# Hybrid pooling and RG-LRU block with a mixture of experts: the last two experts added by slots on chip, the other rows read back and stored under them

## The chip, the cores and the metric

The kernel runs on one core of a Trainium2 chip. The metric is the device time in microseconds (us) of one execution; the median of three runs of the kernel before is 685.51 us (685.21 to 685.75).

## The reference

One decoder block on 512 tokens of 1024 channels, all in float32. The first part (norm, input projection, pooling mixer, recurrence, gates, output projection) gives `x`; the change does not touch it. What it touches is the mixture of experts and the last norm. Of 4 groups of 4 experts each token gets the best group and in it the best 2 experts, with the weights `comb` (512 by 16); an expert goes from 1024 channels to 512 and back. `rms_norm` is x times rsqrt(mean(x*x) + 1e-6) times the factors.

```python
def hier_moe(h, rg_w, rg_b, re_w, re_b, e_gate, e_up, e_down):
    ...
    comb = jnp.einsum('tk,tke->te', w2, jax.nn.one_hot(ids, N_EXP, dtype=jnp.float32)).astype(h.dtype)
    y = jnp.zeros_like(xt)
    for e in range(N_EXP):
        he = jax.nn.silu(xt @ e_gate[e]) * (xt @ e_up[e])
        y = y + comb[:, e:e + 1] * (he @ e_down[e])
    return y.reshape(b_, s_, d_)

def reference(...):
    ...
        x = x + (g_a * y_a + g_b * y_b) @ w_out[l]
        h2 = rms_norm(x, norm2_g[l])
        x = x + hier_moe(h2, ...)
    return rms_norm(x, norm_f_g)
```

## The kernel before, in words

**Slots.** Each expert has 128 slots, one per partition. `rows[:, e]` holds the token of each slot (a number from 512 up for an empty one, which every indirect transfer with its bounds check leaves out), `wslot[:, e]` its weight. With 512 tokens, 2 experts each and 16 experts, a slot list holds 64 tokens on average. `h2d` in HBM holds the normed rows, `xd` in HBM is the accumulator that the block's `x` is written to and every expert's result is added to.

**An expert.** GpSimd gathers the expert's rows of `h2d` into `xg` (`gather`, L507). TensorE transposes them (`x_parts`, L776); a float32 is carried as a high and a low part (`evac4`, L502: ACT copies the high part, DVE subtracts for the low), and each product is three matmuls (`tok_mm`, L784). `gate_half` and `up` (L840, L823) make 128x512 results, `hidden` (L793) the silu product, `h_parts` (L799) its transposed parts `ht`, `down` (L831) the 128x1024 result, which ACT scales into `yt`. `scatter_add` (L805) adds `yt` into `xd` by an indirect DMA of GpSimd. The loop at L849 interleaves: expert `e`'s gate halves stand around expert `e-1`'s `h_parts`, then `down(e-1)`, then `up(e)`.

**Weights.** They come in chunks of 1 MB in the order of the list `chunks` (L122 to L131) over SyncE's queue, three in flight (`load_raw`, L138). A chunk is split in two halves into high and low parts (`split`, L150: ACT copies, DVE subtracts), always three halves ahead of their use (`weights`, L159). Raw chunks and split halves share the 20 buffers of the tag `b8`; one half is one buffer, and one raw chunk too.

**Order.** The framework places instructions on each engine by a list: first what stands first in the program, as soon as its plan says it is ready. On an engine the order is then fixed, and each instruction waits in place for its semaphores. An `If` block is one unit in that list. Its body here (L881 to L934) works off experts with more than 128 tokens and is skipped with these inputs; every engine loads the count `nmi`, branches, and puts the semaphores of the skipped body right.

**The last two experts and the end.** Expert 14's second `down` half stands behind expert 15's `up` (L858 to L875), expert 14's scatter behind it. Then the overflow test (L880), then the read-back of all of `xd` into `xb` (L937 to L939), the load of the last norm's factors `gfb`, expert 15's `h_parts` and products (L944 to L951). Expert 15's result does not go through `xd`: a 0/1 matrix `back` (slots by tokens, L866 to L873) spreads it over the 512 rows by 16 matmuls, DVE adds them to `xb`, ACT makes sums of squares, GpSimd the power -0.5, and DVE (ACT and GpSimd for two parts) scales and hands each half row block to a store (L957 to L980).

Of the kernel before, what the change touches and what calls it, by code (L numbers as in the profile page):

```python
# [8 lines left out]
F32 = mybir.dt.float32  # L9
F32R = mybir.dt.float32r  # L10
# [7 lines left out]
P = 128  # L18
# [18 lines left out]
def tile_hybrid_block(  # L37
# [469 lines left out]
    def gather(idx, dst, n=S):  # L507
        return POOL.indirect_dma_start(  # L508
            out=dst, out_offset=None, in_=h2d[:n, :],
            in_offset=bass.IndirectOffsetOnAxis(ap=idx, axis=0),  # L510
            bounds_check=n - 1, oob_is_err=False).ins
# [335 lines left out]
    L = NE - 1  # L847
    hh = None
    for e in range(NE):  # L849
# [16 lines left out]
    toki = s2([P, S], I32, "toki")  # L866
    POOL.iota(toki, pattern=[[1, S]], base=0, channel_multiplier=0)
    tokf = s2([P, S], F32, "tokf")
    DVE.tensor_copy(tokf, toki)
    slf = tiny([P, 1], F32, "slf", 1)  # L870
    DVE.tensor_copy(slf, rows[:, L:L + 1])
    back = s2([P, S], F32R, "back")
    DVE.tensor_scalar(back, tokf, slf, None, op0=ALU.is_equal)  # L873
    for _ in part:
        pass  # L875
    for i in range(2):
        weights(c_d[L][i], 0, 0)


    n_max = nc.values_load(nmi[0:1, 0:1], min_val=0, max_val=S)  # L880
    with tc.If(n_max > P):  # L881
        emp = s2([P, S * NE // P], I32, "emp")
        POOL.iota(emp, pattern=[[1, S * NE // P // NE], [0, NE]], base=0, channel_multiplier=S // P)
        DVE.tensor_scalar(emp, emp, P - 1, None, op0=ALU.bitwise_and)
        DVE.tensor_scalar(emp, emp, S, None, op0=ALU.add)
        POOL.dma_start(tbl.rearrange("(p n) o -> p (n o)", p=P), emp)
        emw = s2([P, S * NE // P], F32, "emw")
        POOL.memset(emw, 0.0)
        POOL.dma_start(tblw.rearrange("(p n) o -> p (n o)", p=P), emw)
        ids = tiny([P, NT], I32, "ids", 1)  # L890
        POOL.iota(ids, pattern=[[P, NT]], base=0, channel_multiplier=1)
        adi = tiny([P, NT, 2], I32, "adi", 1)
        DVE.tensor_copy(adi, addr)
        for t in range(NT):
            for k in range(2):
                off = bass.IndirectOffsetOnAxis(ap=adi[:, t, k:k + 1], axis=0)
                POOL.indirect_dma_start(out=tbl, out_offset=off, in_=ids[:, t:t + 1], in_offset=None)
                POOL.indirect_dma_start(out=tblw, out_offset=off, in_=wtok[:, t, k:k + 1], in_offset=None)
        with tc.For_i(0, NE, 1) as ie:
            with tc.For_i(P, S, P) as iq:  # L900
                sl = const.tile([P, 1], I32, name="osl")
                SP.dma_start(sl, tbl.rearrange("(s n) o -> s (n o)", n=NE)[bass.ds(iq, P), bass.ds(ie, 1)])
                wsl = const.tile([P, 1], F32, name="owsl")
                SP.dma_start(wsl, tblw.rearrange("(s n) o -> s (n o)", n=NE)[bass.ds(iq, P), bass.ds(ie, 1)])
                og = s4([P, D], F32, "og")
                POOL.memset(og, 0.0)
                gather(sl, og)
                xt = b8([P, 2, KD, P], F32R, "xt_o")
                tb1 = bank("o_t")
                x_parts(og, xt, "o", tb1)  # L910
                r = b8([P, 4, 512], F32, "oraw")
                ow = [b8([P, 2, 2, 512], F32R, f"ow{i}") for i in range(2)]
                ht = s4([P, 2, 4, P], F32R, "ht_o")
                opg, opu = bank("opg"), bank("opu")

                def part(w, r0, c0):
                    src = w[bass.ds(ie, 1), r0:r0 + 512, c0:c0 + 512]
                    SP.dma_start(r, src.rearrange("o (k p) n -> p (o k) n", p=P))
                    for h in range(2):
                        split(r[:, 2 * h:2 * h + 2], ow[h][:, 0], ow[h][:, 1])  # L920
                    return lambda h: ow[h]

                for w, ps in ((e_gate, opg), (e_up, opu)):
                    for i in range(2):
                        tok_mm(ps, xt, 4 * i, part(w, 512 * i, 0), i == 0, i == 1)
                oh_ = hidden(opg, opu, "o")
                for q in range(4):
# [83 lines left out]
```

## Time and profile before

| | |
|---|---|
| median of three runs | 685.51 us (685.21 to 685.75) |
| the profiled execution's own time | 686.77 us |
| its span, first to last instruction | 684.9 us |
| TensorE (PE), busy share of the span | 95% |
| DVE | 73% |
| ACT | 63% |
| GpSimd (POOL) | 11% |
| mean granted TensorE clock | 0.978 |
| HBM read, written | 146.67 MB, 14.16 MB |

PE is TensorE's matmul, PEld its weight load, SP SyncE; a q behind an engine's name is its sequencer. A matmul's end is modelled, so a busy TensorE is read by the distance between starts, and by the shares of stretches rather than of the span. Rows of the chain give start, duration and what held the chain; rows of a line give duration (least/median/most, ns) and the first and last start; "idle before" names what the engine waited for.

### The profile page before, as it was taken

Reading aid. Unit: us, or ns where it says so; the run is one execution under the profiler, and the core shown is the slowest. Engines: PE = TensorE matmul, PEld = TensorE weight load, DVE = VectorE, ACT = ScalarE, POOL = GpSimd, SP = SyncE. Lnnn points to the kernel's source line nnn. Section 1 sums busy time; section 2 is a strip of 40 time slices with the busy share of each in tenths; the row PEclk is TensorE's granted clock in tenths of the full one; section 3 lists DMA queues with packets and bytes.
Section 4 is the critical chain, followed back from the end, with each engine's and each line's share of the span. In section 5 each row is a group of like instructions: output and inputs, shape, how many; then the busy total and the mean of one; then the engine's idle time right before and its main releaser. Section 6 shows DMA issues by size and latency. Waiting matters only on the chain. (4 is left out here: it accounts for less than half of the span.)

```text
span 684.9 us, 8419 instructions
## 1 busy us (share of the span) xinstructions
PE 650.5 (95%) x3044; PEld 528.2 (77%) x3044; DVE 501.8 (73%) x795; ACT 430.9 (63%) x581; POOL 76.5 (11%) x100
## 2 busy tenths in 40 slices
PE   4999999999999999999999999999999999999960
PEld 3788788888888888887777888777777778788850
DVE  5895689972233117657678999898888888889946
ACT  5689958661223224332135888888888888888913
POOL 3000000000100000001120112222222222211013
PEclk9999999999999999999987999999999999999995
DMA  6930321512307131697595899999999999999534
GB/s 202 331 115 1 128 72 35 211 63 76 114 2 250 57 122 68 242 345 263 175 359 185 283 351 350 354 337 339 332 345 346 341 337 340 335 331 344 206 102 162
DMA packets 88052, 153.23 MB, mean 224 GB/s; under 512 B 7249, under 2 KB 29893, under 8 KB 88008
## 3 DMA queue, kind: packets, MB, share of 16 engines
q1 hardware_dynamic: 81736, 138.98, 58.7%
q0 software_dynamic: 5824, 12.64, 6.7%
q10 hardware_dynamic: 448, 1.05, 0.4%
q8 instruction: 24, 0.39, 0.2%
q14 instruction: 20, 0.16, 0.1%
HBM read 146.67 MB, written 14.16 MB: 235 GB/s over the span
## 5 line engine op out<-in xcount | busy, mean ns | idle before, releaser
L152 DVE TENSOR_TENSOR w<-raw,w 128x1024 fp32r<-128x1024 f32 x248 | 293.4, 1220 | 67.4 <-ACT w L151 64.9
L151 ACT CAST w<-raw 128x1024 fp32r<-128x1024 f32 x248 | 249.1, 1051 | 57.3 <-DVE w L152 13.9
L789 PE MATMUL pg<-w,xt 128*128 128x512 f32 x128 | 53.2, 415 | 1.3
L789 PE MATMUL pu<-w,xt 128*128 128x512 f32 x128 | 51.3, 401 | 0.0
L790 PE MATMUL pu<-w,xt 128*128 128x512 f32 x128 | 50.9, 398 | 0.0
L790 PE MATMUL py<-w,ht 128*128 128x512 f32 x128 | 50.8, 397 | 0.0
L790 PE MATMUL pg<-w,xt 128*128 128x512 f32 x128 | 50.5, 394 | 0.0
L791 PE MATMUL pg<-w,xt 128*128 128x512 f32 x128 | 50.5, 394 | 0.0
L791 PE MATMUL pu<-w,xt 128*128 128x512 f32 x128 | 50.1, 392 | 0.0
L791 PE MATMUL py<-w,ht 128*128 128x512 f32 x128 | 49.9, 390 | 0.0
L508 POOL DMA_INDIRECT xg<-h_rows,rows x16 | 27.1, 1694 | 201.3 <-PE xtp L781 173.8
L789 PE MATMUL py<-w,ht 128*128 128x512 f32 x128 | 48.2, 391 | 1.0 <-ACT ht L504 1.0
L789 PEld LDWEIGHTS pg<-w,xt 128*128 128x128 f32 x128 | 24.3, 190 | 10.1 <-ACT w L151 5.9
L806 POOL DMA_INDIRECT x_acc<-y,rows x15 | 24.5, 1633 | 55.3 <-ACT y L836 51.6
L790 PEld LDWEIGHTS pg<-w,xt 128*128 128x128 f32 x128 | 24.4, 190 | 6.6 <-DVE w L152 0.7
L789 PEld LDWEIGHTS py<-w,ht 128*128 128x128 f32 x128 | 24.0, 188 | 6.2 <-ACT ht L504 1.3
L790 PEld LDWEIGHTS pu<-w,xt 128*128 128x128 f32 x128 | 24.1, 188 | 5.7 <-DVE w L152 0.2
L791 PEld LDWEIGHTS pg<-w,xt 128*128 128x128 f32 x128 | 24.3, 189 | 5.0
L791 PEld LDWEIGHTS py<-w,ht 128*128 128x128 f32 x128 | 24.1, 188 | 5.0 <-DVE ht L505 0.4
L791 PEld LDWEIGHTS pu<-w,xt 128*128 128x128 f32 x128 | 24.0, 188 | 4.7
L789 PEld LDWEIGHTS pu<-w,xt 128*128 128x128 f32 x128 | 24.0, 188 | 4.6
L790 PEld LDWEIGHTS py<-w,ht 128*128 128x128 f32 x128 | 24.1, 188 | 4.5
(303 smaller groups left out, 1408.9 us busy)
## 6 DMA issues: line engine op xcount, KB each, us to landing
raw<-in_exp_w_gate_dram SPq DMA_DIRECT2D x32, 1024.0 KB
raw<-in_exp_w_up_dram SPq DMA_DIRECT2D x32, 1024.0 KB
raw<-in_exp_w_down_dram SPq DMA_DIRECT2D x32, 1024.0 KB
raw<-in_w_in_dram SPq DMA_DIRECT2D x17, 1024.0 KB
raw<-in_proj_b_dram SPq DMA_DIRECT2D x4, 1024.0 KB
raw<-in_w_out_dram SPq DMA_DIRECT2D x4, 1024.0 KB
x_rows<-in_x_dram SPq DMA_DIRECT2D x4, 512.0 KB
xrow<-in_x_dram SPq DMA_DIRECT2D x4, 512.0 KB
```

Source lines behind the costliest of these rows:

```text
L151: ACT.copy(hi, r)
L152: DVE.tensor_tensor(lo, r, hi.bitcast(F32), op=ALU.subtract)
L508: return POOL.indirect_dma_start(out=dst, out_offset=None, in_=h2d[:n, :], in_offset=bass.IndirectOffsetOnAxis(ap=idx, axis=0), bounds_che ...
L789: PE.matmul(ps, hi, w[:, 0, k % 2, :], start=first and k == 0, stop=False)
L790: PE.matmul(ps, hi, w[:, 1, k % 2, :], start=False, stop=False)
L791: PE.matmul(ps, lo, w[:, 0, k % 2, :], start=False, stop=last and k == 3)
L806: POOL.indirect_dma_start(out=xd, out_offset=bass.IndirectOffsetOnAxis(ap=idx, axis=0), in_=src, in_offset=None, bounds_check=S - 1, oob_i ...
```

## The change

The weights of expert 14's second `down` half go back to their regular place. The overflow block moves, unchanged, into a function that is called in the loop at expert 14, behind `down(13)` and `next_x(15)` and ahead of `up(14)`. Behind it `read_back` loads the 512 rows of `xd` (experts 0 to 13 added) into `xb`, and gathers expert 14's and expert 15's rows of `xd` by their slots into `xz`. `rows_in_both` makes a 0/1 matrix `same` (slots of 14 by slots of 15 that hold one token) and `rows_m`, which is `rows` of expert 14 with the tokens that are in both lists moved out of bounds. Expert 14's result is kept on chip: added to its `xz` by GpSimd, and through four matmuls with `same` to expert 15's `xz`. Expert 15's up product goes in two column halves, its down product in two row halves between them. The 512 rows are normed and stored, behind the last split on ACT and DVE; then both `xz` are normed and stored over them by two indirect DMAs of GpSimd, which wait for the four row stores.

```diff
@@ chunks
-        if e == NE - 1:
-            late = chunks.pop()
         add_exp(c_u, e_up, e, False)
-    c_d[NE - 2][1] = len(chunks)
-    chunks.append(late)
     add_exp(c_d, e_down, NE - 1, True)
@@ split
+    latest = [None, None]
     def split(r, hi, lo):
-        ACT.copy(hi, r)
-        DVE.tensor_tensor(lo, r, hi.bitcast(F32), op=ALU.subtract)
+        latest[0] = ACT.copy(hi, r).ins
+        latest[1] = DVE.tensor_tensor(lo, r, hi.bitcast(F32), op=ALU.subtract).ins
@@ gather takes its source as src=h2d
@@ before the loop over the experts
+    def overflow():
+        n_max = nc.values_load(nmi[0:1, 0:1], min_val=0, max_val=S)
+        with tc.If(n_max > P):
...
+    def read_back():
+        xzt = b8([P, 2, D], F32, "xz")
+        POOL.memset(xzt, 0.0)
+        for i in range(2):
+            xb[i] = b8([P, 2, D], F32, f"xb{i}")
+        for t in range(NT):
+            SP.dma_start(xb[t // 2][:, t % 2, :], xd[t * P:(t + 1) * P, :])
+        for i in range(2):
+            xz[L - 1 + i] = xzt[:, i, :]
+            gather(rows[:, L - 1 + i:L + i], xz[L - 1 + i], src=xd)
+        gfb = const.tile([P, D], F32, tag="c4", name="gfb")
+        gl = SP.dma_start(gfb, norm_f_g.unsqueeze(0).to_broadcast([P, D])).ins
+        tc.add_manual_dep(gl, loads[len(chunks) - 1].name, SYNC, reason="after the last weights")
+        return gfb
+    def rows_in_both():
+        DVE.tensor_copy(rowsf, rows[:, L - 1:L + 1])
+        tp = bank("rowst")
+        PE.transpose(tp[:, :P], rowsf[:, 1:2].to_broadcast([P, P]), ident)
+        DVE.tensor_scalar(same, tp[:, :P], rowsf[:, 0:1], None, op0=ALU.is_equal)
+        both = tiny([P, 1], F32, "both", 1)
+        DVE.reduce_sum(both, same.bitcast(F32), axis=AX.X)
+        DVE.scalar_tensor_tensor(both, both, float(S), rowsf[:, 0:1], op0=ALU.mult, op1=ALU.add)
+        DVE.tensor_copy(rows_m, both)
+    def finish_rows(z, idx, nm):
+        rs = rstd_of(z, nm)
+        DVE.scalar_tensor_tensor(z, z, rs, gfb, op0=ALU.mult, op1=ALU.mult)
+        over = POOL.indirect_dma_start(
+            out=outr, out_offset=bass.IndirectOffsetOnAxis(ap=idx, axis=0),
+            in_=z, in_offset=None, bounds_check=S - 1, oob_is_err=False).ins
+        for st in stores:
+            tc.add_manual_dep(over, st.name, SYNC, reason="over the rows stored first")
@@ loop over the experts
         gate_half(e, pg, 1)
-        if e > 0:
-            part = down(e - 1, ht)
-            next(part)
         if 0 < e < L:
-            for _ in part:
+            for _ in down(e - 1, ht):
                 pass
             next_x(e + 1)
-        hh = hidden(pg, up(e), f"{e}")
+        if e == L - 1:
+            overflow()
+            gfb = read_back()
+            rows_in_both()
+        if e < L:
+            hh = hidden(pg, up(e), f"{e}")
@@ behind the loop: the code from L866 on is replaced
+    for n in range(2):
+        c = slice(n * 512, (n + 1) * 512)
+        py = bank(f"py{L - 1}_{n}")
+        tok_mm(py, ht, 0, exp_w(c_d[L - 1], n), True, True)
+        ACT.activation(yt[:, c], py, AF.Copy, scale=wslot[:, L - 1:L])
+        ACT.copy(yp[:, 0, c], yt[:, c])
+        POOL.tensor_tensor(yp[:, 1, c], yt[:, c], yp[:, 0, c].bitcast(F32), op=ALU.subtract)
+        POOL.tensor_tensor(xz[L - 1][:, c], xz[L - 1][:, c], yt[:, c], op=ALU.add)
+    def share():
+        for n in range(2):
+            c = slice(n * 512, (n + 1) * 512)
+            ps = bank(f"share{n}")
+            for j in range(2):
+                PE.matmul(ps, same, yp[:, j, c], start=j == 0, stop=j == 1)
+            DVE.tensor_tensor(xz[L][:, c], xz[L][:, c], ps, op=ALU.add)
...
+    for i in range(2):
+        up_part(0, i)
+    hidden_part(0)
+    with tc.issue_after(up_last[0]):
+        up_part(1, 0)
+    turn_part(0)
+    up_part(1, 1)
+    hidden_part(1)
+    weights(c_d[L][1], 0, 0)
+    down_part(0, 0)
+    turn_part(1)
+    down_part(0, 1)
+    stores = []
+    with tc.issue_after(latest[0]), tc.issue_after(latest[1]):
+        for t in range(NT):
+            xv = xb[t // 2][:, t % 2, :]
+            rs = rstd_of(xv, f"f{t}")
+            DVE.scalar_tensor_tensor(xv, xv, rs, gfb, op0=ALU.mult, op1=ALU.mult)
+            stores.append(SP.dma_start(outr[t * P:(t + 1) * P, :], xv).ins)
+    share()
+    for n in range(2):
+        down_part(1, n)
+    for n in range(2):
+        c = slice(n * 512, (n + 1) * 512)
+        DVE.scalar_tensor_tensor(xz[L][:, c], py[n], wslot[:, L:L + 1], xz[L][:, c], op0=ALU.mult, op1=ALU.add)
+    finish_rows(xz[L - 1], rows_m, "fz0")
+    finish_rows(xz[L], rows[:, L:L + 1], "fz1")
```

In this listing `rstd_of` (L210) is one ACT square with its sum, a small DVE step and a power on GpSimd. `up_part(c, i)` makes 256 of the 512 columns; the new `hidden_part`, `turn_part` and `down_part(c, n)` do for half of the columns or rows what `hidden`, `h_parts` and `tok_mm` do for all.

## Rows read from the trace of the kernel before

**Rows 1.** The page's busy time, share of the span and instructions of each engine.

```profile
PE 650.5 (95%) x3044; PEld 528.2 (77%) x3044; DVE 501.8 (73%) x795; ACT 430.9 (63%) x581; POOL 76.5 (11%) x100
```

**Rows 2.** Busy time by stretch, count in brackets; then TensorE's clock, DMA share, GB/s.

```profile
640.00:650.00 10.00, 10.00 (x46) 8.26 (x44) 10.00 (x11) 9.57 (x12) 0.00 (x0) 1.00 0.33 131
650.00:660.00 10.00, 8.82 (x39) 6.63 (x38) 6.25 (x9) 1.97 (x3) 1.92 (x1) 1.00 0.20 29
670.00:680.00 10.00, 0.00 (x0) 0.00 (x0) 8.70 (x19) 5.24 (x14) 5.36 (x6) 0.50 0.25 95
```

**Rows 3.** The chain that ended last: start, duration, what held it.

```profile
663.87 6.98 DMA xb<-x_acc
...
674.25 1.11 POOL frs L970 x2
```

**Rows 4.** The overflow test's line: sequencer instructions, least/median/most ns, first and last start.

```profile
L881 SPq EVENT_SEMAPHORE  x8: 17/17/17, 645.2 to 648.4; - x8
L881 POOLq EVENT_SEMAPHORE  x5: 17/43/5686, 655.2 to 661.2; - x5
...
L881 PEldq EVENT_SEMAPHORE  x1: 51/51/51, 653.4 to 653.4; - x1
...
L881 POOLq INC_SWDGE_SEM  x1: 1080/1080/1080, 661.3 to 661.3; - x1
```

**Rows 5.** Timelines of GpSimd, DVE and SyncE: start, duration, instruction, idle before.

```profile
631.22 1.55 POOL L806 DMA_INDIRECT x_acc<-y,rows  x1 [15.67 <-ACT y L836]
...
654.34 1.92 POOL L806 DMA_INDIRECT x_acc<-y,rows  x1 [20.96 <-ACT y L836]
...
632.89 4.63 DVE L152 TENSOR_TENSOR w<-raw,w 128x1024 fp32r<-128x1024 f32 x4
...
644.28 0.34 SPq L941 DMA_DIRECT2D gfb<-in_norm_f_g_dram  x1
```

**Rows 6.** Timeline of TensorE's matmuls: a dense row, a gap, and four short ones.

```profile
649.77 0.39 PE L789 MATMUL pu<-w,xt 128*128 128x512 f32 x1
...
652.94 0.39 PE L791 MATMUL py<-w,ht 128*128 128x512 f32 x1
...
655.14 0.50 PE L789 MATMUL py<-w,ht 128*128 128x512 f32 x1 [1.03 <-ACT ht L504]
...
304.65 0.63 PE L556 MATMUL lg<-xt,rwr 128*64 128x256 f32 x4
305.12 0.40 PE L722 MATMUL po<-w,mt 128*128 128x512 f32 x1
```

**Rows 7.** DVE: one row of splits, then durations of three lines.

```profile
642.04 8.03 DVE L152 TENSOR_TENSOR w<-raw,w 128x1024 fp32r<-128x1024 f32 x7
...
L566 DVE SCALAR_TENSOR_TENSOR h<-x,rs_n,g2b x3: 1276/1279/1283, 309.0 to 340.1; 128x1024 f32<-128x1024 f32 x3
...
L796 DVE TENSOR_TENSOR silu<-silu,pu x16: 680/681/682, 385.1 to 651.5; 128x512 f32<-128x512 f32 x16
...
L979 DVE SCALAR_TENSOR_TENSOR xb<-xb,frs,gfb x6: 737/748/1747, 674.9 to 680.8; 128x512 f32<-128x512 f32 x6
```

**Rows 8.** Timeline of GpSimd: a two-input product of 512 columns.

```profile
676.79 1.26 POOL L977 TENSOR_TENSOR xb<-xb,gfb 128x512 f32<-128x512 f32 x1
```

**Rows 9.** ACT's square with its sum, and GpSimd's power, by line.

```profile
L213 ACT ACTIVATE sq_n<-x x3: 1057/1057/1057, 306.7 to 337.8; 128x1024 bf16<-128x1024 f32 x3
L213 ACT ACTIVATION_READ_ACCUMULATOR sq_n<-x x3: 186/186/186, 307.7 to 338.8; 128x1 f32 x3
...
L217 POOL TENSOR_TENSOR rs_n<-ms_n,mhalf x7: 549/560/571, 5.7 to 339.5; 128x1 f32<-128x1 f32 x7
```

**Rows 10.** The last stores, SyncE's drain, and the gathers' landing by line.

```profile
L980 SPq DMA_DIRECT2D out_dram<-xb x6: 332/332/338, 675.6 to 681.6; - x6
...
L1006 SPq DRAIN  x3: 7/7/13, 684.0 to 684.3; - x3
...
DMA to landing us min/median/max: 4.3/7.9/8.4
```

More of the change, by code (lines that the diff above doesn't have):

```diff
@@ new lines, in tile_hybrid_block @@
+    xb = [None, None]
+    xz, rowsf, same = {}, tiny([P, 2], F32, "rowsf", 1), const.tile([P, P], F32R, name="same")
+    rows_m = tiny([P, 1], I32, "rowsm", 1)
+    def read_back():
[12 more added lines that the diff above has]
+        return gfb
@@ L871, in tile_hybrid_block @@
[L871 to L927, printed above, removed]
-                    PE.transpose(tb1[:, q * P:(q + 1) * P], oh_[:, q * P:(q + 1) * P], ident)
-                evac4(tb1, ht[:, 0], ht[:, 1])
-                for n in range(2):
-                    ps = (opg, opu)[n]
-                    tok_mm(ps, ht, 0, part(e_down, 0, 512 * n), True, True)
-                    ACT.activation(og[:, n * 512:(n + 1) * 512], ps, AF.Copy, scale=wsl)
-                scatter_add(sl, og)
@@ L937, in tile_hybrid_block @@
-    xb = [b8([P, 2, D], F32, f"xb{i}") for i in range(2)]
-    for t in range(NT):
-        SP.dma_start(xb[t // 2][:, t % 2, :], xd[t * P:(t + 1) * P, :])
-    gfb = const.tile([P, D], F32, tag="c4", name="gfb")
-    gl = SP.dma_start(gfb, norm_f_g.unsqueeze(0).to_broadcast([P, D])).ins
-    tc.add_manual_dep(gl, loads[len(chunks) - 1].name, SYNC, reason="after the last weights")
-    ht = s4([P, 2, 4, P], F32R, f"ht{L}")
-    h_parts(hh, ht, f"{L}")
-    ssum = [tiny([P, 2], F32, f"fss_{t}", 4) for t in range(NT)]
@@ new lines, in tile_hybrid_block, with up_part @@
+    sg = s2([P, DE], F32, f"silu{L}")
+    ACT.activation(sg, pg, AF.Silu)
+    pu = [bank(f"pu{L}_{c}") for c in range(2)]
+    htp = bank(f"htp{L}")
+    ht = s4([P, 2, 4, P], F32R, f"ht{L}")
+    py = [bank(f"py{L}_{n}") for n in range(2)]
+    up_last = [None]
+    def up_part(c, i):
+        for h in range(2):
+            w = exp_w(c_u[L], i)(h)
+            for kk in range(2):
+                k = 4 * i + 2 * h + kk
+                hi, lo = xts[L][:, 0, k, :], xts[L][:, 1, k, :]
+                w_h, w_l = (w[:, j, kk, 256 * c:256 * c + 256] for j in range(2))
+                PE.matmul(pu[c][:, :256], hi, w_h, start=k == 0, stop=False)
+                PE.matmul(pu[c][:, :256], hi, w_l, start=False, stop=False)
+                up_last[0] = PE.matmul(pu[c][:, :256], lo, w_h, start=False, stop=k == KD - 1).ins
@@ new lines, in hidden_part, with turn_part @@
+    def hidden_part(c):
+        s = sg[:, 256 * c:256 * c + 256]
+        DVE.tensor_tensor(s, s, pu[c][:, :256], op=ALU.mult)
+    def turn_part(c):
+        for q in range(2 * c, 2 * c + 2):
+            PE.transpose(htp[:, q * P:(q + 1) * P], sg[:, q * P:(q + 1) * P], ident)
+        tv = htp[:, 256 * c:256 * c + 256].rearrange("p (q s) -> p q s", q=2)
+        qs = slice(2 * c, 2 * c + 2)
+        ACT.copy(ht[:, 0, qs], tv)
+        DVE.tensor_tensor(ht[:, 1, qs], tv, ht[:, 0, qs].bitcast(F32), op=ALU.subtract)
@@ new lines, in down_part @@
+    def down_part(c, n):
+        w = exp_w(c_d[L], n)(c)
+        for kk in range(2):
+            k = 2 * c + kk
+            hi, lo = ht[:, 0, k, :], ht[:, 1, k, :]
+            PE.matmul(py[n], hi, w[:, 0, kk, :], start=k == 0, stop=False)
+            PE.matmul(py[n], hi, w[:, 1, kk, :], start=False, stop=False)
+            PE.matmul(py[n], lo, w[:, 0, kk, :], start=False, stop=k == 3)
+    for i in range(2):
+        up_part(0, i)
+    hidden_part(0)
+    with tc.issue_after(up_last[0]):
+        up_part(1, 0)
@@ new lines, in tile_hybrid_block @@
+    turn_part(0)
[7 more added lines that the diff above has]
+    with tc.issue_after(latest[0]), tc.issue_after(latest[1]):
+        for t in range(NT):
+            xv = xb[t // 2][:, t % 2, :]
[3 more added lines that the diff above has]
+    share()
```

89 lines of the change are left out of this document (51 added, 38 removed).

## The prediction, before the change was run

> **What bounds the kernel now.** I read the page's busy line first [rows 1], then the table by stretch [rows 2], then the chain that ended last [rows 3], then single lines. The reader is to see two kernels in one. Up to about 653 us the expert stream runs: TensorE is busy 10.00 of the 10 us from 640 to 650, and so is DVE (10.00), with ACT at 9.57; nobody has room. Behind it lies a tail: from 670 to 680 TensorE does nothing and the DMA engines are a quarter busy [rows 2]. The chain [rows 3] says why. Expert 14's rows are scattered into the accumulator in HBM at 654.34 [rows 5]. GpSimd, skipping the overflow body, waits 5.69 us until that scatter has landed (661.2) and then needs 1.08 us to put the count of its queue right [rows 4]. Only then do the four loads of `xb` start; they hold the chain for 6.98 us, and the adds, squares, powers, products and stores of all 512 rows follow. TensorE's second to last dense stretch ended at 653.17 (the row at 652.94 plus one step), the span at 684.9: 31.7 us of tail, in which expert 15's own 24 matmuls take 5.4.
>
> **Part 1: the read-back goes forward.** The chain scatter of expert 14, landing, 1.08 us, read-back, adds is gone: the 512 rows are read after expert 13's scatter, which starts at 631.22 [rows 5]. With the landing time of the scatter at 654.34 (6.9 us) and the 1.08 us, GpSimd is through the skipped body at about 639.2; the 1.08 us are still paid, with nobody waiting. SyncE has its own part: in before it spends 645.2 to 648.4 on eight semaphore steps of the skipped body [rows 4], right behind the load of `gfb` at 644.28, which waits for the last weights [rows 5]. So the loads of `xb` start between 639 and 648, and behind the wait on SyncE only they, the stores and perhaps the last weights are queued. Four loads in the 6.98 us of [rows 3], shared with two gathers, land by 655 at the latest. Their users come after the last split, so this is covered, with next to no slack at the late end.
>
> **Part 2: TensorE's order.** Fifteen matmuls of 512 columns start from 649.77 to 652.94 [rows 6], 0.226 us each. The reordered stretch (gate 15, down 14, up 15) keeps its work. Up 15 becomes 48 matmuls of 256 columns instead of 24 of 512. Four of 256 take the 0.47 us between two rows of [rows 6], 0.118 us each: 48 x 0.118 = 5.66 against 24 x 0.226 = 5.42, +0.24 us. The overflow test drains TensorE once before and once after, so that is moved, not added. The gap of 1.03 us ahead of expert 15's first product [rows 6] is what the half-wise order is meant to fill. Then 24 products (5.42), 4 for `share` (0.90) and transposes (about 0.5): 653.17 + 0.24 + 6.8 + 0.3 for waits on splits gives 660.5; one column pass of up 15 now wants four split halves in 2.8 us while DVE makes one in 1.15, so I allow 1 us more: 661.5. The 16 products with `back` are gone.
>
> **Part 3: DVE, the engine that becomes the bound.** At 642.04 DVE starts an unbroken row of splits, 7 in 8.03 us, 1.147 each [rows 7]. By the order of the chunks ten halves are left there (two of down 14, four of up 15, four of down 15): 11.5 us. After that it must do, before the last product is finished: four half-width steps of `hidden_part` and `turn_part` (half of the 0.681 us of [rows 7], say 0.37 each, 1.5); four rows products at 1.28 (5.1) with a tenth each for their small step (0.4); two `share` adds at 0.68 (1.4); two final products at 0.75 (1.5). The five small steps of `rows_in_both` are weighed against the three removed for `back`, at nothing. Sum: 642.04 + 11.5 + 1.5 + 5.5 + 1.4 + 1.5 = 663.4.
>
> To this comes contention. The change gives GpSimd four two-input operations of 512 columns (`yp` low parts, `xz` adds) between about 647 and 657, where DVE is full. In before two such ran, 1.26 us [rows 8], and the DVE product beside one took 1.747 us against a median of 0.748 [rows 7]: 1.0 us lost each time. Bounds: 0 (all fall beside PSUM reads or gaps) to 4 x 1.0 = 4.0; I take 3.0, nearer the row, since splits read two SBUF tiles like that product. Final product: 666.4. The Trainium skill (Advanced Engine Details and Errata, VectorE Performance Modes) says that GpSimd and two-port Vector instructions block each other over a shared port; the row agrees. By that rule taken in full the sum would be 1 us higher, with the port free it would be 3 us lower. For the five powers, of one column each, I add nothing.
>
> **Part 4: the new ending.** After the final product: ACT's square of 1024 columns, 1.057 + 0.186 [rows 9]; the small DVE step and three hand-overs, about 0.35; the power on an idle DVE port, 0.56 [rows 9]; the product, 1.28 [rows 7]. The other overwriting set's product of 1.28 fits into DVE's wait. 666.4 + 1.24 + 0.35 + 0.56 + 1.28 = 669.8. Then the indirect store of some 64 rows. Before has no plain scatter. From below stands the fastest gather of such rows, 4.3 us to landing [rows 10], from above the adding scatter at 654.34, 6.9 us [rows 4, 5]. I take 5.5, the middle, since it writes to HBM like the second but reads nothing there. The Trainium skill (DMA: Bandwidth & Descriptors, Anatomy of one DMA) gives 2.0 us plus the bytes for such a transfer; for 64 rows and an issue of 1.9 us that would be an estimated 4.5 us, and the sum 1 us less; no run so far shows it. The span ends 0.9 us after SyncE's drain at 684.0 [rows 10]. So 669.8 + 0.2 + 5.5 + 0.9 = 676.4, 8.5 us before the 684.9 of before. The timed median is 0.6 above that span (the profiled execution's own time 1.9 above); I move the median by the same 8.5: **677.0**.
>
> What is queued behind the new waits: on GpSimd the first overwriting store waits for the four row stores. If it stands ahead of the second set's power, that power and all after it wait. The rows are finished at about 660.5 + 3 = 663.5, and a store of 256 KB takes 2.4 us (681.6 to 684.0 [rows 10]); four of 512 KB are down by about 668, when the power is due (668.0). So this costs 0 to 2 us, and nothing in the sum.
>
> **The rivals.**
> A. TensorE, not DVE, ends last: the port costs nothing, DVE gets ahead, the final product ends at 661.5 + 0.75 = 662.3. Then 662.3 + 3.4 + 5.7 + 0.9 = 672.3, time 672.9. For it speaks that DVE loses some work; against it the 10.00 of [rows 2].
> B. The rows are worked last. DVE takes share adds and final products first, the rows end at 666.4, the stores land some 4.5 us later (670.9), the two indirect stores of 1.9 and 5.5 us follow: 678.3 + 0.9 = 679.2, time 679.8. For it speaks that the rows need ACT, GpSimd and late loads; against it their place in the program, ahead of the share.
> C. The moved test holds up the stream. Its body owns tiles of the same 20 buffers as the weights. If a split's tile takes a buffer whose last owner is the body, ACT and DVE wait until SyncE has passed the body, that is behind the last weights at 644.28, whereas the splits beside the test are due from 632.89 on [rows 5]; the half just behind it about 634.1. The stall is up to 10.2 us in the fullest stretch: 676.4 + 10.2 = 686.6, time 687.2, slower by 0.25%. It decides from 8.5 us of stall on. For it speaks that [rows 4] shows real waits at the skipped body on each engine (TensorE's step at 653.4 comes when its matmuls have drained); against it that in before nothing on ACT or DVE waited more than half a microsecond there, and that six of twenty buffers should be free at that place.
> D. The read-back does not get early (it waits for something of expert 14 after all): the old chain stays, no change, 685.5.
>
> **How the numbers follow.** Forecast 0.53, A 0.22, B 0.12, C 0.10 (half of it short of slower, about no change), D 0.03. The likeliest is 677.0. Its own bounds are contention (-3, +1) and landing (-1.2, +1.4). The range takes in most of A below and B above: 671.5 to 682.5, and leaves out C, D and the odd end, some 0.16. A measurement of this kernel tells 0.2% (1.4 us) from no change; faster by more is forecast, A, B: 0.87; within it half of C and D: 0.06; slower: 0.07.
>
> **What the profile of the changed kernel would show.** Part 1: the loads of `xb` between 639 and 648 and no such load in the closing chain. Part 2: TensorE unbroken to about 661, no gap of 1 us ahead of expert 15's products. Part 3: DVE full from 640 to 666, its splits or row products longer beside the four GpSimd operations; if DVE idles there, A holds. Part 4: the chain ending in final product, square, power, product, indirect store, 10 us altogether. If ACT or DVE stands still for microseconds behind the test line, C holds; if the last overwriting store waits for row stores, B. Wrong would also be a landing of the plain scatter outside 4.3 to 6.9 us.

## The result, and the profile after

The changed kernel takes 703.74 us (median of four runs, 701.18 to 708.0) against 685.36 us for the kernel before in the same comparison: ratio 1.0268, 95% interval 1.0242 to 1.0295. The forecast was 677.0 with a range of 671.5 to 682.5; the kernel is slower, by some 18 us. The profiled execution took 701.18 us, its span is 699.2.

The first view is the table by stretch of the kernel after (busy time of PE, PEld, DVE, ACT and GpSimd with the count of instructions, then TensorE's granted clock, DMA share, GB/s); the rows of before are [rows 2].

```profile
620.00:630.00 10.00, 9.85 (x51) 8.11 (x50) 9.80 (x10) 7.71 (x11) 0.52 (x1) 1.00 0.97 340
630.00:640.00 10.00, 4.15 (x19) 3.06 (x17) 3.18 (x7) 1.82 (x3) 1.04 (x1) 0.95 0.99 322
640.00:650.00 10.00, 2.56 (x6) 2.10 (x7) 2.58 (x3) 3.66 (x4) 3.91 (x3) 0.50 0.59 203
650.00:660.00 10.00, 10.00 (x41) 8.11 (x41) 8.19 (x9) 6.07 (x9) 0.00 (x0) 0.86 0.37 147
```

Where before had every engine full (10.00 for TensorE and DVE from 640 to 650), all of them now stand still together for well over ten microseconds. The timelines of ACT, DVE and TensorE say who waits for whom (start, duration, instruction, in brackets the idle time ahead and what ended it):

```profile
631.55 1.05 ACT L149 CAST w<-raw 128x1024 fp32r<-128x1024 f32 x1 [0.66 <-DVEq L849]
646.34 6.73 ACT L149 CAST w<-raw 128x1024 fp32r<-128x1024 f32 x7 [13.73 <-SPq L849]
...
632.64 1.22 DVE L150 TENSOR_TENSOR w<-raw,w 128x1024 fp32r<-128x1024 f32 x1
647.42 3.50 DVE L150 TENSOR_TENSOR w<-raw,w 128x1024 fp32r<-128x1024 f32 x3 [13.55 <-ACT w L149]
...
647.44 0.80 PE L787 MATMUL pg<-w,xt 128*128 128x512 f32 x1 [13.29 <-ACT w L149]
648.03 0.63 PE L788 MATMUL pu<-w,xt 128*128 128x512 f32 x1
648.46 0.63 PE L789 MATMUL pu<-w,xt 128*128 128x512 f32 x1
```

One copy of one weight half on ACT waits 13.73 us for SyncE's sequencer on line 849, the moved overflow test; DVE waits for that copy, TensorE for both. The test's own line (sequencer instructions with count, least/median/most ns, first and last start), which answers to [rows 4]:

```profile
L849 SPq EVENT_SEMAPHORE  x8: 17/17/17, 643.5 to 646.7; - x8
L849 POOLq EVENT_SEMAPHORE  x5: 17/43/8725, 630.3 to 639.3; - x5
...
L849 ACTq EVENT_SEMAPHORE  x1: 17/17/17, 630.2 to 630.2; - x1
...
L849 DVEq EVENT_SEMAPHORE  x1: 21/21/21, 631.4 to 631.4; - x1
...
L849 SPq COMPARE_BRANCH  x1: 45/45/45, 643.0 to 643.0; - x1
```

ACT is through the skipped body at 630.2 and DVE at 631.4. SyncE comes to its branch only at 643.0, behind the load of `gfb` (issued at 642.64, after 10.2 us of waiting for the last weights), and steps its eight semaphores until 646.7. ACT goes on at 646.34, in the midst of those steps: by the trace's records of semaphores and landings, `gfb` has landed at 646.28, SyncE's third step starts at 646.30, and ACT's copy 0.04 us behind it. The end of the kernel, on GpSimd and in the chain that ended last:

```profile
688.03 1.28 DVE L938 SCALAR_TENSOR_TENSOR xz<-xz,rs_fz,gfb 128x1024 f32<-128x1024 f32 x1 [0.73 <-POOL rs_fz L215]
...
688.41 1.82 POOL L939 DMA_INDIRECT out_dram<-xz,rowsm  x1 [0.42 <-issue]
693.19 0.99 POOL L939 DMA_INDIRECT out_dram<-xz,rows  x1 [2.96 <-DMA out_dram<-xz,rowsm]
...
688.41 3.98 DMA out_dram<-xz,rowsm
```

The second indirect store waits for the landing of the first (3.98 us from its start).

**A measure for the stage.** Expert 13's scatter is the last event ahead of the change. In the profiled executions of this case it starts anywhere from 628.4 to 633.8 us, so the traces are compared from its start to the end of the span: before 684.9 - 631.22 = 53.7 us, after 699.2 - 629.49 = 69.7 us, 16.0 more. A stage is that of one execution (after's is the fastest of its four, x4's the slowest of its ten), so a difference of a microsecond between two stages says little by itself. The ratios of the medians stand beside it.

### The profile page after: what moved, and what is told of

It reads as the page before. It is cut to its first block, busy times and chain, and to the rows that moved or that the text cites. A ratio compares the mean times of both kernels' runs of the same rounds, so it can differ in the third digit from the quotient of the medians.

```text
span 699.2 us, 8454 instructions
## 1 busy us (share of the span) xinstructions
PE 652.1 (93%) x3057; PEld 531.0 (76%) x3057; DVE 502.3 (72%) x791; ACT 430.9 (62%) x576; POOL 84.5 (12%) x107
## 5 line engine op out<-in xcount | busy, mean ns | idle before, releaser
L150 DVE TENSOR_TENSOR w<-raw,w 128x1024 fp32r<-128x1024 f32 x248 | 296.4, 1232 | 82.5 <-ACT w L149 80.3
L787 PE MATMUL pg<-w,xt 128*128 128x512 f32 x128 | 53.8, 420 | 14.5 <-ACT w L149 13.3
L787 PE MATMUL pu<-w,xt 128*128 128x512 f32 x120 | 48.4, 403 | 0.0
L788 PE MATMUL pu<-w,xt 128*128 128x512 f32 x120 | 48.4, 403 | 0.0
L788 PE MATMUL py<-w,ht 128*128 128x512 f32 x120 | 47.7, 398 | 0.0
L789 PE MATMUL pu<-w,xt 128*128 128x512 f32 x120 | 47.5, 396 | 0.0
L789 PE MATMUL py<-w,ht 128*128 128x512 f32 x120 | 46.7, 389 | 0.0
L787 PE MATMUL py<-w,ht 128*128 128x512 f32 x120 | 45.0, 390 | 0.0
L788 PEld LDWEIGHTS pu<-w,xt 128*128 128x128 f32 x120 | 22.9, 191 | 5.5 <-DVE w L150 0.2
L804 POOL DMA_INDIRECT x_acc<-y,rows x14 | 22.5, 1608 | 34.3 <-ACT y L834 30.7
L720 PE MATMUL po<-w,mt 128*128 128x512 f32 x64 | 26.4, 413 | 0.0
L789 PEld LDWEIGHTS pu<-w,xt 128*128 128x128 f32 x120 | 22.8, 190 | 4.5
L787 PEld LDWEIGHTS py<-w,ht 128*128 128x128 f32 x120 | 22.5, 188 | 4.7
L787 PEld LDWEIGHTS pu<-w,xt 128*128 128x128 f32 x120 | 22.7, 189 | 4.3
L503 DVE TENSOR_TENSOR xt<-xtp,xt 128x512 fp32r<-128x512 f32 x30 | 19.3, 684 | 9.2 <-ACT xt L502 9.2
```

The source lines that it names most:

```text
L150: latest[1] = DVE.tensor_tensor(lo, r, hi.bitcast(F32), op=ALU.subtract).ins
L503: DVE.tensor_tensor(lo, tv, hi.bitcast(F32), op=ALU.subtract)
L720: PE.matmul(po, a_h, w_h, start=k == 0, stop=False)
L787: PE.matmul(ps, hi, w[:, 0, k % 2, :], start=first and k == 0, stop=False)
L788: PE.matmul(ps, hi, w[:, 1, k % 2, :], start=False, stop=False)
L789: PE.matmul(ps, lo, w[:, 0, k % 2, :], start=False, stop=last and k == 3)
```

## The experiments

Two theories on the stall stood at first. Theory A: the waiting split waits for the count of a DMA queue on which the skipped body's loads count too, a matter of the loads. Theory B, which is rival C of the prediction: its tile lies in a buffer that a tile of the body owned last. All twelve results together:

| kernel | stage, us | ratio to before, 95% interval |
|---|---|---|
| before | 53.7 | 1 |
| after | 69.7 | 1.0268, 1.0242 to 1.0295 |
| e1, no test | 52.6 | 0.9990, 0.9976 to 1.0005 |
| e6, before with the test moved | 67.4 | 1.0175, 1.0150 to 1.0199 |
| e3, `gfb` behind the test | 66.7 | 1.0214, 1.0172 to 1.0257 |
| x1, body without weight buffers | 54.9 | 1.0005, 0.9993 to 1.0018 |
| x3, `oraw` in another buffer | 53.8 | 1.0007, 0.9992 to 1.0022 |
| x4, x3 and first set early | 52.5 | 0.9972, 0.9954 to 0.9989 |
| x5, x3 and four operations on DVE | 52.5 | 0.9960, 0.9943 to 0.9976 |
| x8, x4 and x5 and splits ahead | 52.4 | 0.9978, 0.9958 to 0.9998 |
| x9, x5 and `gfb` behind the test | 54.9 | 0.9996, 0.9971 to 1.0022 |
| x10, x9 and first set early | 54.2 | 0.9988, 0.9967 to 1.0008 |
| x11, x10 and splits ahead | 50.8 | 0.9939, 0.9920 to 0.9958 |
| x12, x11 and rows earlier | 48.4 | 0.9927, 0.9907 to 0.9947 |

**e1_no_test** is the kernel after without the overflow block, so the work of slots past 128 is left out.

```diff
         if e == L - 1:
-            overflow()
             gfb = read_back()
```

> The changed kernel without the overflow block (it leaves out the work for experts with more than 128 tokens). Theory: the loss is the wait of ACT behind the moved test, 13.7 us at the split of expert 14's up weights, plus 11 matmuls at 0.43 instead of 0.23 us after it; both go, and 701.2 falls to about 685. Rival 1: the new ending itself (column halves, indirect stores one after the other) costs more than the old tail, with or without the test: still above 690. Rival 2 (my forecast's sum holds once the test is out): 675 to 679.

Measured: 685.13 us against 685.82, ratio 0.999. Of after's stage 17.1 us go with the test. But the gain that was forecast for the rest is not there either: a second question.

**e6_before_test_moved** is the kernel before with nothing but the block moved.

```diff
         gate_half(e, pg, 1)
+        if e == L - 1:
+            overflow()
...
-    n_max = nc.values_load(nmi[0:1, 0:1], min_val=0, max_val=S)
-    with tc.If(n_max > P):
-        ...
```

> The kernel before with the overflow block alone moved to where the change has it; nothing else. Theory: the same wait of ACT for SyncE's passage of the skipped body appears, 13 to 14 us, and the time goes from 685.4 to about 699 to 702. Rival (the loss belongs to the new ending): within 2 us of 685.

Measured: 697.62 us, ratio 1.0175; the stage is 13.7 us longer than before's. ACT's timeline:

```profile
647.07 4.83 ACT L151 CAST w<-raw 128x1024 fp32r<-128x1024 f32 x5 [13.14 <-SPq L850]
```

The same wait, 13.14 us. Moving the test alone brings it, whatever the rest of the change does.

**e3_gfb_behind** lets the load of `gfb` wait for the last load of `xb`, so that SyncE comes to its branch earlier.

```diff
-            SP.dma_start(xb[t // 2][:, t % 2, :], xd[t * P:(t + 1) * P, :])
+            xl = SP.dma_start(xb[t // 2][:, t % 2, :], xd[t * P:(t + 1) * P, :]).ins
...
-        tc.add_manual_dep(gl, loads[len(chunks) - 1].name, SYNC, reason="after the last weights")
+        tc.add_manual_dep(gl, xl.name, SYNC, reason="after the read-back")
```

> The changed kernel, but the load of the last norm's factors waits for the last load of the read-back, so that it stands behind the test on SyncE and not ahead of it. Theory (ACT waits for SyncE's passage, and SyncE's passage for everything that it has in flight): SyncE reaches the test at 632.5 instead of 643 and is through when the last weights have landed, about 642.5 instead of 646.7; ACT's stall shrinks by 3 to 5 us, the time to about 697. Rival (ACT waits for something else of the body, a buffer or GpSimd's passage): no change, 701.

Measured: 700.32 us, ratio 1.0214; the stage is 3.0 us shorter than after's, ACT's wait 1.7 us shorter:

```profile
649.01 6.74 ACT L149 CAST w<-raw 128x1024 fp32r<-128x1024 f32 x7 [12.05 <-SPq L849]
```

SyncE's branch is now at 638.5, its semaphore steps still only from 646.4 to 649.4: with `gfb` gone, the passage itself waits until the weight loads that SyncE has issued are down (the last two landed at 646.36 and 648.95, the steps for them start at 646.37 and 648.97). What holds ACT is SyncE's passage up to the last such landing, and the place of `gfb` decides little of it. These are two executions, and the ratio's interval overlaps after's, so the gain in time is not settled; the wait is read from the trace.

**x1_body_no_b8** keeps the test, both loops, the two small SyncE loads, gather and scatter of the body, and leaves out its products and all its tiles in the 20 weight buffers (slots past 128 would only be scaled and added).

```diff
-                    xt = b8([P, 2, KD, P], F32R, "xt_o")
-                    ...
-                    r = b8([P, 4, 512], F32, "oraw")
-                    ow = [b8([P, 2, 2, 512], F32R, f"ow{i}") for i in range(2)]
-                    ...
+                    POOL.tensor_scalar(og, og, wsl, None, op0=ALU.mult)
```

> The changed kernel with an overflow body that uses none of the 20 weight buffers: its loops and two small loads on SyncE stay, its weight loads, splits and matmuls are left out. Theory A (a wait for a load's semaphore, which SyncE has to put right when it skips the body): a stall of ACT stays, though shorter, 7 to 11 us, because only two of eight semaphores are the body's: 693 to 698. Theory B (a split takes a buffer that the body owned, as in rival C of the prediction): no stall, as without the test.

Measured: 686.38 us, ratio 1.0005. ACT's eight copies beside the test run in one piece:

```profile
631.01 7.67 ACT L149 CAST w<-raw 128x1024 fp32r<-128x1024 f32 x8
```

SyncE's branch is as late as ever (644.2), and ACT does not wait for it: theory A, which expected 7 to 11 us of stall here, falls, and the stall hangs on what was left out, the body's tiles or the loads into them. (SyncE's passage has only two steps here instead of eight, and the next run puts the eight back.)

**x3_oraw_apart** is the kernel after with the whole body. Only its raw weight tile, the one that SyncE's loads write, takes the buffer of `xb0`, which SyncE writes next anyway.

```diff
     def overflow():
+        xb[0] = b8([P, 4, 512], F32, "xb0")
...
-                    r = b8([P, 4, 512], F32, "oraw")
+                    r = xb[0]
...
-        for i in range(2):
-            xb[i] = b8([P, 2, D], F32, f"xb{i}")
+        xb[0] = xb[0].rearrange("p (t h) n -> p t (h n)", t=2)
+        xb[1] = b8([P, 2, D], F32, "xb1")
```

> The whole kernel after, with one edit: the body's weight tile oraw is no tile of its own any more; the body writes into the first read-back buffer, xb0, which is taken just ahead of the test and whose next writer is SyncE's own read-back. Theory (buffer last owned by the body): the split behind the test no longer waits for SyncE's passage, the 13.7 us of waiting on ACT go, and the time is that of the kernel without the test, 685.1 (684 to 687). Rival 1 (a passage of the body by any engine holds the split, through ow or xt_o): a wait of ten microseconds or more stays on ACT and the time is 700 or above. Rival 2 (the body's mere size holds up the code): 690 to 700 with the wait spread over several engines.

Measured: 686.08 us, ratio 1.0007; against after, 2.6% come back with the full work.

```profile
630.97 7.70 ACT L149 CAST w<-raw 128x1024 fp32r<-128x1024 f32 x8 [0.66 <-DVEq L850]
...
L850 SPq EVENT_SEMAPHORE  x8: 17/17/17, 645.7 to 652.0; - x8
```

So it is one tile. SyncE's passage is there in full, eight steps to 652.0, and ACT has done its eight copies long before: the counts of the queues alone hold nobody. The reading that fits all runs is that the split behind the test took the buffer that `oraw` owned last, on SyncE's account, and had to wait for SyncE. Which buffer the split got is in no view, and the edit takes `xb0`'s buffer earlier as well; no run does that alone. The 0.66 us that are left on ACT wait for DVE's passage, and x1, without the body's other tiles, does not have them. The next runs ask where the forecast gain went. The view that raises the question is the trace of e1, where the stall is absent (DVE, GpSimd, ACT and TensorE, then DVE and GpSimd at the end):

```profile
650.68 6.44 DVE L150 TENSOR_TENSOR w<-raw,w 128x1024 fp32r<-128x1024 f32 x3 [0.24 <-ACT w L149]
...
651.56 2.28 POOL L973 TENSOR_TENSOR yp<-y,yp 128x512 fp32r<-128x512 f32 x1
653.79 2.25 POOL L974 TENSOR_TENSOR xz<-xz,y 128x512 f32<-128x512 f32 x1
...
644.42 0.69 ACT L971 ACTIVATE y<-py,wslot 128x512 f32<-128x512 f32 x1 [2.12 <-PE py L789]
...
657.51 0.44 PE L1011 MATMUL htp<-ident,silu 128*128 128x128 f32 x2 [3.28 <-DVE silu L1007]
...
667.52 1.40 DVE L1053 SCALAR_TENSOR_TENSOR xz<-py,wslot,xz 128x512 f32<-128x512 f32 x2
...
671.79 1.28 DVE L938 SCALAR_TENSOR_TENSOR xz<-xz,rs_fz,gfb 128x1024 f32<-128x1024 f32 x1 [0.73 <-POOL rs_fz L215]
...
676.95 0.99 POOL L939 DMA_INDIRECT out_dram<-xz,rows  x1 [2.96 <-DMA out_dram<-xz,rowsm]
```

Splits take 2.15 us each beside GpSimd's operations, GpSimd's own take 2.25 instead of the 1.26 of [rows 8], an evacuation at the head of ACT's queue keeps the splits from ACT for 2.12 us, and the last store starts 3.9 us after its rows are ready.

**x4_first_set_early**: x3, with the overwriting set of expert 14 finished ahead of the share.

```diff
+    finish_rows(xz[L - 1], rows_m, "fz0")
     share()
...
-    finish_rows(xz[L - 1], rows_m, "fz0")
     finish_rows(xz[L], rows[:, L:L + 1], "fz1")
```

> As x3_oraw_apart, and the overwriting set of expert 14 is finished and stored ahead of the share, not behind the final products. Theory (the second indirect store waits for the landing of the first, 2.96 us seen, and both stand behind the last products): the first is issued by about 670 instead of 672.2, the second within 0.5 us of its product; 2 to 4 us off x3_oraw_apart, 681 to 683.5. Rival (the first store is held by the four row stores, whose landing is at about 670, and the wait moves there): 0 to 1.5 us off.

Measured: 684.4 us, ratio 0.9972, some 2.4 us below x3 by the ratios and 1.3 by the stage. GpSimd's timeline:

```profile
674.22 1.04 POOL L940 DMA_INDIRECT out_dram<-xz,rowsm  x1 [4.46 <-DVE xz L1056]
675.29 0.58 POOL L215 TENSOR_TENSOR rs_fz<-ms_fz,mhalf 128x1 f32<-128x1 f32 x1
678.21 1.03 POOL L940 DMA_INDIRECT out_dram<-xz,rows  x1 [2.34 <-DMA out_dram<-xz,rowsm]
```

The first store's set was ready at 671.7, and it still goes at 674.2. The profile puts its wait down to DVE, whose last product ended at 673.7, but the trace's own records name the row stores: the last one, issued at 670.58, landed at 673.29, GpSimd's wait for that landing ended at 673.31, and the store starts 0.9 us later, as it does behind the same wait in x11 and x12. The gain is between theory and rival: the chain of stores (rows, first set, second set) is in series, and the early product only shortens it.

**x5_four_on_dve**: x3, with GpSimd's four two-input operations on DVE.

```diff
-        POOL.tensor_tensor(yp[:, 1, c], yt[:, c], yp[:, 0, c].bitcast(F32), op=ALU.subtract)
-        POOL.tensor_tensor(xz[L - 1][:, c], xz[L - 1][:, c], yt[:, c], op=ALU.add)
...
+    for n in range(2):
+        c = slice(n * 512, (n + 1) * 512)
+        DVE.tensor_tensor(yp[:, 1, c], yt[:, c], yp[:, 0, c].bitcast(F32), op=ALU.subtract)
+        DVE.tensor_tensor(xz[L - 1][:, c], xz[L - 1][:, c], yt[:, c], op=ALU.add)
     stores = []
```

> As x3_oraw_apart, with the four two-input operations (low parts of yp, adds into xz) moved from GpSimd to DVE, 0.68 us each by rows of that size. Theory (GpSimd's operations slow the splits over a shared resource): the splits there go back from 1.6 to 2.3 us each to 1.15 to 1.22; 3.3 us are won and 2.7 us of work are added, so x3_oraw_apart less 0.6 (685.1 - 0.6 = 684.5, 683 to 685.5). Rival (the splits are slow because the read-back fills SBUF at the same time): they stay slow, and the added work makes it x3_oraw_apart plus 2.7, about 688.

Measured: 683.24 us, ratio 0.996 (0.9943 to 0.9976): faster than before, and 1.3 (stage) to 3.2 us (ratios) below x3. DVE's splits of x3, then those of x5:

```profile
646.55 11.27 DVE L150 TENSOR_TENSOR w<-raw,w 128x1024 fp32r<-128x1024 f32 x6 [1.51 <-ACT w L149]
```

```profile
645.80 2.36 DVE L150 TENSOR_TENSOR w<-raw,w 128x1024 fp32r<-128x1024 f32 x2 [0.26 <-ACT w L149]
648.08 0.69 DVE L1041 TENSOR_TENSOR xz<-xz,y 128x512 f32<-128x512 f32 x1
648.68 4.63 DVE L150 TENSOR_TENSOR w<-raw,w 128x1024 fp32r<-128x1024 f32 x4
```

Six splits take 11.27 us beside GpSimd and 6.99 us without: 4.3 us, or 1.07 for each of the four operations. The read-back is not the cause: x5 has it too, from 651.0, and its splits take 1.16 us; in x3 it is asked for at 652.3, and splits ahead of it already take 2.27 us each:

```profile
647.70 4.54 DVE L150 TENSOR_TENSOR w<-raw,w 128x1024 fp32r<-128x1024 f32 x2
```

The trace agrees with the rule of the Trainium skill that the prediction named (Advanced Engine Details and Errata, VectorE Performance Modes), in both directions: in x3 GpSimd's four operations take 8.7 us, 3.6 more than at 1.26 each, and DVE's splits 4.3 more.

**x8_all**: x4 and x5 together, and four halves split ahead of `down` 14.

```diff
+    weights(c_d[L - 1][1], SPLIT_AHEAD + 1, RAW_AHEAD)
     for n in range(2):
```

> x4_first_set_early and x5_four_on_dve together, and four split halves asked for ahead of down 14, so that ACT makes them where it stood idle for 2.1 us with an evacuation at the head of its queue (DVE then waited 1.4 us). Theory (the three losses are separate): 3 us for the early store, 0.6 for GpSimd, 1.4 for ACT's order off x3_oraw_apart: about 680 (678 to 682.5). Rival (one engine, DVE, is full in any case, and what is won ahead of the last split is lost in its queue behind it): no better than x4_first_set_early by more than 0.5 us.

Measured: 683.87 us, ratio 0.9978, stage 52.4: the rival. DVE splits without a gap, ten in 11.44 us, and then waits:

```profile
656.88 0.42 DVE L1016 TENSOR_TENSOR ht<-htp,ht 128x256 fp32r<-128x256 f32 x1 [2.25 <-ACT ht L1015]
...
660.59 0.69 DVE L1042 TENSOR_TENSOR xz<-xz,y 128x512 f32<-128x512 f32 x1 [2.68 <-DMA xz<-x_acc,rows]
```

ACT's `ht` copy stands behind squares that wait 2.66 us for `xb`; and `xb` is asked for only at 650.70, because SyncE's passage waits until `gfb`, issued ahead of it, is down (landed at 650.05). The second wait is for the first gather of `xz`, whose instruction alone took 10.28 us on GpSimd.

**x9_gfb_behind**: x5 with the edit of e3.

> As x5_four_on_dve, and the load of gfb waits for the last load of xb, so that it stands behind the test on SyncE's queue. Theory (SyncE's passage of the skipped body waits for the landing of whatever it issued ahead, here gfb, 5.3 us of waiting on its own branch line; ACT's squares then wait 1.9 us for xb and expert 15's cast ht stands behind them in ACT's queue): xb is asked for by about 645 instead of 651.0, the 1.9 us waits on ACT and DVE go, and 1.5 to 2.5 us come off x5_four_on_dve: 680.7 to 681.7. Rival (TensorE, half clocked there, ends last in any case): within 0.5 us of x5_four_on_dve, 683.2.

Measured: 686.65 us, ratio 0.9996, 2.5 us worse than x5 by the ratios, 2.4 by stage. A miss, and an instructive one.

```profile
645.40 1.79 SPq L917 DMA_DIRECT2D xb<-x_acc  x4
...
654.89 0.69 DVE L1041 TENSOR_TENSOR xz<-xz,y 128x512 f32<-128x512 f32 x1 [4.48 <-DMA xz<-x_acc,rows]
655.50 4.62 DVE L150 TENSOR_TENSOR w<-raw,w 128x1024 fp32r<-128x1024 f32 x4
```

`xb` came early as foretold. But its 2 MB now run beside GpSimd's two gathers of `xz`: from issue to landing these take 8.8 us where x5 has 6.0 (medians of the two). The records of the first gather divide the difference. Its instruction ends at 648.0, and from there to the landing it takes 6.8 us against 3.2 in x5, nearly all of it beside the read-back; x8 and x10, likewise beside it, have 6.9 and 6.8, and x3 and x4, whose read-back starts later, and x12, where it is down by then, 3.2 to 3.3. The instruction itself takes 3.1 us against 1.7, and what stretches it (10.3 in x8, 10.9 in x12) no run settles. One add into `xz` stands in DVE's queue ahead of the last splits, and DVE waits 4.48 us for it. TensorE, out of weights, is granted half its clock from 655 to 660 (0.50).

**x10_gfb_early** is x9 with the first set early, **x11_gfb_all** that with the halves ahead (the edits of x4 and x8).

> As x9_gfb_behind, and the overwriting set of expert 14 finished and stored ahead of the share. Theory (with the rows stored earlier the first indirect store can go at about 667 and has landed when the second set is ready; GpSimd's power of the second set no longer stands behind the first store): the second store starts within 0.5 us of its product, 2 to 3 us off x9_gfb_behind less the 1.28 us by which the first set's product now precedes the last products on DVE: 1 to 2 us off, about 679.5. Rival (the first store is still held by the row stores' landing): no gain.

> As x10_gfb_early, with four split halves asked for ahead of down 14 (x8_all with gfb behind the read-back). Theory: DVE's splits end about 1 us earlier (they ran unbroken in x8_all, 641.21 to 652.65) and the four moved operations stand behind them where DVE waited; another 0 to 1 us off x10_gfb_early. Rival (the four operations then hold share and the rows back): 0.5 to 1.5 us above x10_gfb_early.

Measured: x10 685.89 us, ratio 0.9988, with the same wait in DVE's queue (4.47 us); x11 682.71 us, ratio 0.9939 (0.9920 to 0.9958), 3.4 us below x10. In x11 the four moved operations stand behind the splits, which run without a gap, and no add waits for a gather:

```profile
642.14 11.43 DVE L150 TENSOR_TENSOR w<-raw,w 128x1024 fp32r<-128x1024 f32 x10
...
657.63 0.68 DVE L1042 TENSOR_TENSOR xz<-xz,y 128x512 f32<-128x512 f32 x1
```

x8 has the same order and still waited 2.68 us, because its first gather landed only at 660.5 (in x11 at 648.6). The expectation for x10 missed for the reason of x9; that for x11 was too small because it took the cause for ACT's order alone.

**x12_rows_before_turn**: x11 with the block of the rows' statistics, products and stores (and the four moved operations) written ahead of `turn_part(1)`.

```diff
     down_part(0, 0)
+    for n in range(2):
+        ...
+    stores = []
+    ...
     turn_part(1)
     down_part(0, 1)
```

> As x11_gfb_all, with the statistics and products of the 512 rows written ahead of expert 15's second turn, so that DVE does the last add into xz and the small steps of the rows where it waited 2.17 us for that turn's cast. Theory (DVE ends the kernel: what moves into its idle time comes off the end): the rows' products start about 1 us earlier, and so do the row stores, the first indirect store that waits for their landing, and the end: 1 us off x11_gfb_all by the ratio to before, 0.9925 (0.991 to 0.994). Rival (the second indirect store, held by the landing of the first, is set by the row stores alone and these stay where they are): the same ratio as x11_gfb_all, 0.994.

Measured: 680.81 us (679.62 to 681.47) against 686.01, ratio 0.9927 (0.9907 to 0.9947). The stage is 48.4 us, 5.3 below before's. DVE, then GpSimd:

```profile
641.65 11.43 DVE L150 TENSOR_TENSOR w<-raw,w 128x1024 fp32r<-128x1024 f32 x10
...
660.05 4.87 DVE L1046 SCALAR_TENSOR_TENSOR xb<-xb,rs_f,gfb 128x1024 f32<-128x1024 f32 x4 [0.19 <-POOL rs_f L215]
...
668.80 1.04 POOL L940 DMA_INDIRECT out_dram<-xz,rowsm  x1 [3.13 <-DVE xz L1059]
...
672.80 1.03 POOL L940 DMA_INDIRECT out_dram<-xz,rows  x1 [1.76 <-DVE xz L939]
```

The rows' products start 29.6 us after the scatter of expert 13, in x11 32.0, and the stores behind them come forward with them. The profile puts the second store's wait down to its own product, which ended at 672.4; but the first store landed at 672.0 by the trace's records, and the second starts 0.8 us after that, the same distance as in x3, x4 and x11. So the series of row stores, first set and second set still sets the end. This version has the whole computation and is 0.7% faster than the kernel before. Against x11 the intervals overlap, and the gain is read from the stage, 2.4 us.

## Why the prediction was wrong, point by point

The step that failed is the moved test: the sum has no term for a wait behind it, on the ground that no such wait showed in before and that buffers should be free. It measured 13.7 us on ACT. Without it the sum was still 7.4 us too low, mainly in DVE's waits and in the second of the two indirect stores.

**Rival C decided, and was priced too low.** The mechanism stood there, with a chance of 0.10 and a price of 10.2 us of stall. Three things in it failed. First the price: it ended the wait at 644.28, where SyncE comes to its branch. The wait ends inside SyncE's passage, when what SyncE has in flight has landed, and how long the passage takes was in view in [rows 4], eight steps up to 648.4 in before. From the second half behind the test (632.6 in after) to 646.34 it measured 13.73. With that in place of 10.2 the rival's 687.2 becomes about 690.7, and all of it lies on the slow side, where half of its chance was counted as no change. Second the argument from before, that nothing on ACT or DVE waited there for more than half a microsecond: there the last splits were behind the engines, so no split could be caught. A row from a place where the mechanism cannot act is no evidence against it. Third, that six of twenty buffers should be free: what counts is whose buffer the next tile gets, and by the reading of x3 that was `oraw`'s.

**The 17.1 us between after and e1, added up.** DVE's first split comes 0.8 us later after expert 13's scatter; the stall takes 13.6 on DVE; from there to the end of the final products after needs 37.7 us and e1, from the same split, 35.1, 2.6 more; the ending is alike (0.1). The 2.6 are waits of DVE for TensorE, ACT and GpSimd (5.9 us in sum against 2.9 in e1, while its last splits take 0.6 less), with TensorE at half clock: 0.50 of the full 2.4 GHz from 640 to 650, after nothing had started on it for 13.3 us, its matmuls 0.43 us apart against the 0.226 of [rows 6].

**Without the stall the forecast was still 7.4 us too low.** It gave a span of 676.4, or 675.5 on e1's time (whose stage starts 0.94 us earlier); e1's is 682.9.
- Part 1 held in its effect (the loads of `xb` at 646.85 in after and 647.17 in e1, no read-back in the closing chain). Its landing was late: the last load was down at 658.1 in e1, not by 655, and ACT's squares waited 1.02 us for one.
- Part 2 is neither shown nor refuted as the bound: its 48 narrow products cost 0.12 us each as reckoned while its clock was full. TensorE was not unbroken to 661 as foretold: it waits for DVE (3.28 us ahead of expert 15's first transposes), and behind that wait its products come 0.43 us apart, with a granted clock of 0.78 in the mean of 660 to 665.
- Part 3, DVE as the bound, was right; its sum was 3.4 us short (final products done at 668.9 against 665.5). Contention was taken at 3.0, from one slowed row of before: the seven last splits of e1 took 11.75 us against 7 x 1.147 = 8.0, so 3.7; x5 against x3 says 4.3. The rest, 2.9 us, are waits that a sum of busy times leaves out: 1.44 behind ACT's evacuation, 0.24, 0.63 and 0.57; other terms were 0.2 too high together.
- Part 4: from the final products to the last rows' product 4.15 us against 3.4, as the first set's product and power stand between. From there to the end 9.8 us against 6.6. The landing was overrated (4.0 and 3.2 us measured, below the lower bound of 4.3). The Trainium skill (DMA: Bandwidth & Descriptors, Anatomy of one DMA) gave an estimated 4.5, nearer than my 5.5, and the measurement is lower still. But the second store started 3.9 us after its product, behind the landing of the first. The working saw the row stores ahead of the first set and missed the first set ahead of the second: two stores into one tensor were priced as one.

**The other rivals.** A is refuted: DVE idles and yet ends last. B's chain of stores in series is what x4, x8, x11 and x12 end in. D is out: the read-back came early.

## What to carry to other kernels

A skipped block was not free for what stands behind it: a tile of it passed its buffer on only in its owner's passage. So look for the engine that comes to the branch last, price the wait up to the landing of what it has in flight there, and give tiles written by that engine's loads a buffer of which the same engine is the next writer. Where an engine is full, a sum of its busy times needs the waits inside its queue as well, and work on GpSimd beside it was paid for by both here. Moving a transfer forward moves it onto something: ask what is in flight there, and which instruction at the head of a full queue waits for that. And where the profile names one releaser of a wait for several things, compare the landings: here it named DVE where row stores, or the store before, had set the time.

## What the runs showed of the hardware

- SyncE's passage of the skipped block waited for loads that it had issued ahead: 3.1 us of waiting on its branch line in after, 6.3 in x3, 10.2 in x9, each time on to within 0.03 us of a landing. Not for every load: in x1, where the body's weight loads were left out, the passage took two steps and 0.5 us, and `gfb` landed 4.5 us after it.
- A two-input operation of 128x512 on GpSimd took 1.29 us while DVE stood idle (the row below, from after) and 2.25 beside DVE's splits in e1, and each cost DVE 1.07 us (x3 against x5).

```profile
660.76 1.29 POOL L975 TENSOR_TENSOR xz<-xz,y 128x512 f32<-128x512 f32 x1 [15.46 <-ACT y L972]
```

- Plain indirect stores of some 64 rows of 4 KB landed 3.2 to 4.0 us after their start. Gathers of such rows spread far more, from 4.3 us (e3) to 17.2 (x8) for the first of the two, by a longer instruction on GpSimd and, beside the read-back, a later landing.
- TensorE's granted clock was at the lower level, 1.2 GHz, behind the long waits (0.50 in after from 640 to 650, in x9 from 655 to 660), so a stall was paid for a second time in slower matmuls, 0.43 us apart instead of 0.226.
